# Gate and up projections of a feed-forward layer by seven products of half-block sums, tokens on partitions, with the hidden layer kept in DRAM

## The chip, the cores and the metric

The kernel runs on one core of a Trainium2 chip. A core has TensorE for matmuls (PE in the profile, with PEld for its weight loads), VectorE (DVE), ScalarE (ACT), GpSimd (POOL) and SyncE (SP), each with an instruction stream of its own; semaphores tie the streams together. SBUF is the on-chip memory of 128 partitions, PSUM holds matmul results in eight banks of 128 x 512 floats. The metric is device time in microseconds, taken as the median of several executions.

## What is computed

One layer of a decoder on 512 tokens of width 2048, all in float32: RMSNorm, an input projection, four token mixers side by side, an output projection added to the residual, then RMSNorm, a SwiGLU feed-forward of width 5632 and a last RMSNorm. The change lies in the feed-forward and in the last part of the output projection, which prepares its input.

```python
D_MODEL = 2048; SEQ = 512
D_FF = -(-8 * D_MODEL // (3 * 256)) * 256          # 5632
...
def rmsnorm(x, g):
    xf = x.astype(jnp.float32)
    y = xf * lax.rsqrt(jnp.mean(xf * xf, axis=-1, keepdims=True) + NORM_EPS)
    return (y * g.astype(jnp.float32)).astype(x.dtype)
...
        x = x + ycat.reshape(B, S, D_MIX) @ w_out[l]
        h = rmsnorm(x, norm_ffn_g[l])
        x = x + swiglu(h, w_gate[l], w_up[l], w_down[l])
    return rmsnorm(x, norm_final_g)
```

`swiglu(h, g, u, d)` is (silu(h @ g) * (h @ u)) @ d.

## The kernel before

A float32 product is made of three matmuls of a shorter format (F32R): each operand is cut into a high part (a copy on ScalarE that rounds) and a low part (a subtraction on VectorE), and high x high, high x low and low x high are summed in PSUM. Activations have features on partitions and the 512 tokens along the free axis; a tile of 128 x 512 floats comes from one pool of 79 slots (`t2`).

Weights come as one stream of 512 KB chunks in the order of use (`chunks`). `next_chunk` hands out the next one and, before that, issues the loads on SP's queue up to three chunks ahead (`issue_dma`) and the splits up to two ahead (`issue_split`: L122 on ScalarE, L123 on VectorE). A step of `gemm` takes a chunk of 512 input by 256 output features; for each of two blocks of 128 outputs and four slices of the input it gives three matmuls of 128x512, weights stationary and tokens moving (L162, L163, L164). A chunk is thus 24 matmuls. When a block's sum is complete, `on_block` drains it. `gemm_tok` (L180 to L182) is the same with tokens stationary and 512 weights moving. `run` drives these steps, and after each one it lets every generator in the list `side` advance by one step: that is how norms, attention and other side work get their place in the streams. Nothing is reordered later: each engine does what the code issues for it, in that order, with waits where tiles demand them.

The output projection runs in two parts, since the last mixer (attention of mixer A) is still at work: first branches 3, 1 and 2 (`gemm(3, rhs_y, add_x2)`), then branch 0 in eight pairs of blocks of one chunk each. There `split_x2` adds the product to the residual x2 on VectorE (L1030), makes the scaled high part `fh` on ScalarE (L1032), and, one block late, the low part `fl` on VectorE (L1041) and the square on ScalarE (L1047); `add_squares` (L1052) sums squares on VectorE. `ffn_norm` makes 1/rms of each token, spread over a tile R2.

The feed-forward takes the 44 hidden blocks of 128 in groups of eight (the last has four). For each block, `gemm(4, rhs_f, on_gu)` makes gate and up, 96 matmuls, and `on_gu` drains them: gate times R2 on VectorE (L1085), Silu on ScalarE (L1086), up times R2, their product, and the high and low part of it. After a group's blocks `gemm(n // 4, rhs_h, on_dn)` adds the group's share of down to x2, which stays in SBUF. The last group of down is mixed with the final norm, by halves of the tokens.

Of the kernel before, what the change touches and what calls it, by code (L numbers as in the profile page):

```python
# [39 lines left out]
def hybrid_kernel(ctx, tc, xT, wi, wt, wo, wgu, wdn, vec, rows, sgw, w2a2, g2, pbias, cmask, oneh, addc, out):  # L40
# [6 lines left out]
    p1 = ctx.enter_context(tc.tile_pool(name="p1", bufs=8))  # L47
# [7 lines left out]
    def th(name, shape=(128, 4, C)):  # L55
        return p1.tile(list(shape), F32, name=name, tag="sh", bufs=14)

    def t1(name, shape=(128, 8), dt=F32):
        return p1.tile(list(shape), dt, name=name, tag="s1")
# [20 lines left out]
    for g in range(8):  # L80
        chunks.append(wo[g, 0])
    ffg = []
# [5 lines left out]
    for b0, n in ffg:  # L88
        for b in range(b0, b0 + n):
            for kq in range(4):  # L90
                chunks.append(wgu[b, kq])
# [4 lines left out]
    st = dict(dma=0, split=0, use=0)  # L96
    PF, SP = 3, 2

    def issue_dma():
        i = st["dma"]  # L100
        if i >= len(chunks):
            return
# [4 lines left out]
    def issue_split():  # L107
        i = st["split"]
        if i >= len(chunks):
            return  # L110
# [29 lines left out]
    def next_chunk():  # L140
# [3 lines left out]
        while st["dma"] <= min(i + PF + ahead, len(chunks) - 1):  # L144
            issue_dma()
        while st["split"] <= min(i + SP - 1 + ahead, len(chunks) - 1):
# [22 lines left out]
    def gemm_tok(on_tok):  # L169
        """512 output features by all tokens, tokens on partitions; K = 2048."""  # L170
# [49 lines left out]
    class RowNorm:  # L220
        """1 / rms over features, for token columns of feature-major tiles."""
# [68 lines left out]
    def d_block(j, acc):  # L290
        """scale by 1/rms and shift by a token; block j of the RWKV input."""
# [29 lines left out]
    def rwkv_pre():  # L321
# [16 lines left out]
        # decay and in-context learning rate  # L338
# [132 lines left out]
    def turned(name, w):  # L471
        """the transpose of w for each of 8 heads."""
# [8 lines left out]
    def each_head(name, w, m):  # L481
        """w^T m for each of 8 heads (64 x 64 tiles)."""
# [72 lines left out]
    def rwkv_fin(c, gm, LT, dX):  # L555
        """(I - L)^-1 transposed, token-major B|K."""
# [48 lines left out]
    def rwkv_post(c, py3):  # L605
        """group norm per head, bonus, gate."""
# [181 lines left out]
    def attention(mix, br):  # L788
# [11 lines left out]
        class Head:  # L800
# [16 lines left out]
            def scores(self, i):  # L817
                """exp(scores - max) of the 128 queries of block i with their keys."""
# [19 lines left out]
            def turn(self, js):  # L838
                """the weights of key blocks js with keys on partitions."""
# [167 lines left out]
    x2 = []  # L1007
    for g in range(8):
        for b in range(2):
            x2.append(t2("x2"))  # L1010
            nc.scalar.dma_start(x2[-1], xT[:, 2 * g + b, :])
# [5 lines left out]
        def add_x2(b, acc, g=g):  # L1017
            dv.tensor_add(x2[2 * g + b], acc, x2[2 * g + b])
# [5 lines left out]
    fh, fl = [], []  # L1024
    norm2 = RowNorm()
    late = []
# [12 lines left out]
    def low_x2(j):  # L1039
        fl.append(t2("flo", dt=F32R))  # L1040
        dv.scalar_tensor_tensor(fl[j], x2[j], vcol(V_NFG + j), fh[j].bitcast(F32), op0=OP.mult, op1=OP.subtract)  # L1041

    sqs = []

    def square_x2(j):
        sqs.append(t2("sq"))
        ac.activation(sqs[-1], x2[j], AF.Square)  # L1047
# [5 lines left out]

    def ffn_norm():
        while len(sqs) > 1:
            for _ in range(2):
                add_squares()
            yield
# [3 lines left out]
        ac.activation(R2, norm2.spread(), AF.Copy)  # L1062

    for g in range(8):
        run(gemm(1, lambda c, k: (yh[0, k], yl[0, k]),
                 lambda b, acc, g=g: split_x2(g, b, acc)))
    for f in range(4):
        del yh[0, f], yl[0, f]
    R2 = R1

# [1 line left out]
    def rhs_f(c, k):  # L1072
        kt = 4 * c + k
        return fh[kt], fl[kt]

    first = True
    for gi, (b0, n) in enumerate(ffg):
        hh, hl = [], []
        for b in range(n):
            hold = {}  # L1080

            def on_gu(u, acc, b=b, hold=hold):
                if u == 0:
                    gs = hold["g"] = t2("gs")
                    dv.tensor_mul(gs, acc, R2)  # L1085
                    ac.activation(gs, gs, AF.Silu)  # L1086
                    return
                us = t2("us")
                dv.tensor_mul(us, acc, R2)
                dv.tensor_mul(us, us, hold["g"])  # L1090
# [156 lines left out]
```

## Time and profile before

| | us |
|---|---|
| median of 3 runs (2400.09 to 2404.08) | 2400.27 |
| span of the profiled execution | 2402.2 |
| input projection and mixers | 0 to 722.5 |
| output projection, branches 3, 1, 2 | 722.5 to 905.5 |
| output projection, branch 0 (eight pairs of blocks) | 905.5 to 949 |
| feed-forward | 949 to 2343 |
| last group of down and final norm | 2343 to 2402.2 |
| PE busy | 2382.8 (99%) |
| DVE busy | 1038.0 (43%) |
| ACT busy | 702.6 (29%) |

Busy is time with an instruction at work; matmuls overlap in the pipeline, so their distance from start to start is shorter than the length of one. The granted clock stands in the rows as a share of TensorE's full speed.

### The profile page before, as it was taken

Reading aid. Unit: us, or ns where it says so; the run is one execution under the profiler, and the core shown is the slowest. Engines: PE = TensorE matmul, PEld = TensorE weight load, DVE = VectorE, ACT = ScalarE, POOL = GpSimd, SP = SyncE. Lnnn points to the kernel's source line nnn. Section 1 sums busy time; section 2 is a strip of 40 time slices with the busy share of each in tenths; the row PEclk is TensorE's granted clock in tenths of the full one; section 3 lists DMA queues with packets and bytes.
Section 4 is the critical chain, followed back from the end, with each engine's and each line's share of the span. In section 5 each row is a group of like instructions: output and inputs, shape, how many; then the busy total and the mean of one; then the engine's idle time right before and its main releaser. Section 6 shows DMA issues by size and latency. Waiting matters only on the chain.

```text
span 2402.2 us, 28139 instructions
## 1 busy us (share of the span) xinstructions
PE 2382.8 (99%) x11760; PEld 1938.9 (81%) x11760; DVE 1038.0 (43%) x1564; ACT 702.6 (29%) x1016; POOL 2.3 (0%) x16
## 2 busy tenths in 40 slices
PE   8999999999999999999999999999999999999997
PEld 6788878777777778888888888888888888888887
DVE  6555445554445447333333333333333333333337
ACT  5522221225445445222122222222122212222223
POOL 0000000000000000000000000000000000000000
PEclk9999999989999999999999999999999999999999
DMA  5222313213223232233222222232223222322232
GB/s 182 87 89 79 101 56 89 68 53 97 75 75 122 89 105 97 95 98 97 97 97 97 97 97 97 97 98 99 98 93 103 98 97 89 105 97 97 90 120 89
DMA packets 83440, 228.38 MB, mean 95 GB/s; under 512 B 20400, under 2 KB 26032, under 8 KB 83312
## 3 DMA queue, kind: packets, MB, share of 16 engines
q1 hardware_dynamic: 77552, 216.30, 27.6%
q10 hardware_dynamic: 5760, 10.28, 1.4%
q8 instruction: 92, 1.51, 0.2%
q14 instruction: 36, 0.29, 0.0%
HBM read 221.53 MB, written 5.02 MB: 94 GB/s over the span
## 4 chain that ended last, share of the span: by engine, by line
PE 98%; DMA 1%; DVE 1%; ACT 0%; issue 0%; SPq 0%; DVEq 0%
PE acc L162 27%; PE acc L164 26%; PE acc L163 26%; PE acc L180 3%; PE acc L181 2%; PE acc L182 2%; PE po L895 1%; PE psc L830 1%; PE ppt L845 1%; DMA xraw<-in_xT_dram 1%; PE pg L520 1%; PE acc L1153 1%; PE psc L829 1%; PE acc L1154 1%; PE acc L1152 1%; PE py L682 1%
## 5 line engine op out<-in xcount | busy, mean ns | idle before, releaser
L123 DVE TENSOR_TENSOR wlo<-wraw,whi 128x1024 fp32r<-128x1024 f32 x383 | 469.0, 1225 | 784.6 <-ACT whi L122 784.3
L122 ACT ACTIVATE whi<-wraw 128x1024 fp32r<-128x1024 f32 x383 | 404.9, 1057 | 1040.2 <-PE acc L163 834.2
L162 PE MATMUL acc<-fhi,whi 128*128 128x512 f32 x1408 | 548.1, 389 | 0.0
L164 PE MATMUL acc<-fhi,wlo 128*128 128x512 f32 x1408 | 547.9, 389 | 0.0
L163 PE MATMUL acc<-flo,whi 128*128 128x512 f32 x1408 | 547.9, 389 | 0.0
L162 PEld LDWEIGHTS acc<-fhi,whi 128*128 128x128 f32 x1408 | 264.4, 188 | 54.8
L163 PEld LDWEIGHTS acc<-flo,whi 128*128 128x128 f32 x1408 | 264.4, 188 | 54.7
L164 PEld LDWEIGHTS acc<-fhi,wlo 128*128 128x128 f32 x1408 | 264.4, 188 | 54.7
L162 PE MATMUL acc<-hhi,whi 128*128 128x512 f32 x640 | 249.0, 389 | 0.0
L164 PE MATMUL acc<-hhi,wlo 128*128 128x512 f32 x640 | 249.0, 389 | 0.0
L163 PE MATMUL acc<-hlo,whi 128*128 128x512 f32 x640 | 249.0, 389 | 0.0
L162 PE MATMUL acc<-xhi,whi 128*128 128x512 f32 x512 | 211.9, 414 | 4.9 <-ACT whi L137 4.9
L163 PE MATMUL acc<-xlo,whi 128*128 128x512 f32 x512 | 202.8, 396 | 0.7 <-DVE xlo L253 0.7
L164 PE MATMUL acc<-xhi,wlo 128*128 128x512 f32 x512 | 202.8, 396 | 0.6 <-DVE wlo L123 0.6
L163 PEld LDWEIGHTS acc<-hlo,whi 128*128 128x128 f32 x640 | 120.2, 188 | 24.9
L164 PEld LDWEIGHTS acc<-hhi,wlo 128*128 128x128 f32 x640 | 120.2, 188 | 24.9
L162 PEld LDWEIGHTS acc<-hhi,whi 128*128 128x128 f32 x640 | 120.2, 188 | 24.9
L162 PEld LDWEIGHTS acc<-xhi,whi 128*128 128x128 f32 x512 | 97.8, 191 | 30.6 <-ACT whi L137 5.6
L164 PEld LDWEIGHTS acc<-xhi,wlo 128*128 128x128 f32 x512 | 97.8, 191 | 22.9 <-DVE wlo L123 1.8
L163 PEld LDWEIGHTS acc<-xlo,whi 128*128 128x128 f32 x512 | 98.1, 192 | 22.0 <-DVE xlo L253 2.0
L180 PE MATMUL acc<-whi,xhi 128*128 128x512 f32 x256 | 105.2, 411 | 0.0
L162 PE MATMUL acc<-yhi,whi 128*128 128x512 f32 x256 | 103.7, 405 | 0.0
(247 smaller groups left out, 2225.3 us busy)
## 6 DMA issues: line engine op xcount, KB each, us to landing
wraw<-in_wgu_dram SPq DMA_DIRECT2D x176, 512.0 KB, 3.4
wraw<-in_wdn_dram SPq DMA_DIRECT2D x88, 512.0 KB, 3.4
wraw<-in_wi_dram SPq DMA_DIRECT2D x63, 512.0 KB, 3.5
wraw<-in_wt_dram SPq DMA_DIRECT2D x32, 512.0 KB, 3.5
wraw<-in_wo_dram SPq DMA_DIRECT2D x32, 512.0 KB, 3.4
xraw<-in_xT_dram SPq DMA_DIRECT2D x16, 256.0 KB, 5.7
E<-tdram ACTq DMA_DIRECT2D x16, 256.0 KB, 3.6
x<-in_xT_dram ACTq DMA_DIRECT2D x16, 256.0 KB, 2.8
```

The lines of the kernel that those rows point to most:

```text
L122: ac.activation(hi, r, AF.Copy)
L123: dv.tensor_sub(lo, r, hi.bitcast(F32))
L162: pe.matmul(acc[b], wh, xh, start=(c == 0 and k == 0), stop=False)
L163: pe.matmul(acc[b], wh, xl, start=False, stop=False)
L164: pe.matmul(acc[b], wl, xh, start=False, stop=(c == nchunk - 1 and k == 3))
L180: pe.matmul(acc[i], th_, hi[:, k], start=(c == 0 and k == 0), stop=False)
L181: pe.matmul(acc[i], th_, lo[:, k], start=False, stop=False)
L182: pe.matmul(acc[i], tl, hi[:, k], start=False, stop=(c == 7 and k == 1))
L520: pe.matmul(p3[:, u, :], rw.BK[h // 2][q4][rr, ci].rearrange("p a t -> p (a t)"), rw.RA[h // 2][q4][rr, ci].rearrange("p a t -> p (a t)"), ...
L682: pe.matmul(py3[o, h // 2, :], rw.RA[h // 2][c // 4][o, c % 4, 0, :], St[o, h // 2, :], start=False, stop=True)
L829: pe.matmul(o, qs[:, cc], ks[:, 0:n], start=True, stop=False)
L830: pe.matmul(o, qs[self.rr, cc], kl[self.rr, 0:n], start=False, stop=True)
```

## The change

Gate and up are multiplied by Strassen's scheme with seven products of half-size blocks in place of eight. The tokens are cut into two halves of 256, the input features into two halves of eight tiles, and gate and up are the two column halves. Their sums are formed once for the tokens (`combine`, `late_sums`) and for each group of 512 hidden features for the weights (`w_sum`). A product has 256 tokens stationary (two 128-token tiles) and 512 weights moving, over eight tiles of input features: 48 matmuls (L1235 to L1237) in four steps of 12. Eleven groups by seven products by four steps are listed in `steps`; products P1, P6 and P7 go into one chain of PSUM sums. `w_ahead` issues loads, sums and splits of weights two to eight steps ahead. `got_product` drains each product's two token tiles into partial sums; behind P4 the gated second half of the tokens is ready, behind P2 the first half. It now has tokens on partitions, so `turn_h` transposes it on TensorE in two sets of four, copies each on ScalarE and stores it to DRAM (`hd`) from ScalarE's queue. Down then is a stage of its own, which loads h (`load_h`) and x2 (`load_x2`) back and splits h.

In the last part of the output projection, `make_x2` takes the place of `split_x2`: add, scaled copy, store of x2 to DRAM (`xd`) from ScalarE's queue, and a Square that overwrites the tile of x2. Pairs of blocks are now j and j + 8, for which the layout of the weights is changed.

```diff
@@ last part of the output projection
-    def split_x2(g, b, acc):
-        j = 2 * g + b
-        dv.tensor_add(x2[j], acc, x2[j])
-        fh.append(t2("fhi", dt=F32R))
-        ac.activation(fh[j], x2[j], AF.Copy, scale=vcol(V_NFG + j))
-        if j:
-            low_x2(j - 1)
-            square_x2(j - 1)
-        if j % 2:
-            add_squares()
...
+    def make_x2(j, acc):
+        dv.tensor_add(x2[j], acc, x2[j])
+        xg[j] = t2("xg")
+        ac.activation(xg[j], x2[j], AF.Copy, scale=vcol(V_NFG + j))
+        nc.scalar.dma_start(xd[j], x2[j])
+        sqs.append(x2.pop(j))
+        ac.activation(sqs[-1], sqs[-1], AF.Square)
+
+    def split2(hi, src, lo):
+
+        ac.activation(hi, src, AF.Copy)
+        dv.tensor_sub(lo, src, hi.bitcast(F32))
+
+    def combine(j):
+
+        a, b = xg[j], xg[j + 8]
+        s12, s34 = t2("s12"), t2("s34")
+        dv.tensor_add(s12[:, lo_t], a[:, hi_t], b[:, hi_t])
+        dv.tensor_sub(s12[:, hi_t], s12[:, lo_t], a[:, lo_t])
+        gp.tensor_sub(s34[:, lo_t], a[:, lo_t], a[:, hi_t])
+        gp.tensor_sub(s34[:, hi_t], b[:, lo_t], s12[:, hi_t])
+        a11 = t2("a11", dt=F32R)
+        split2(a11[:, lo_t], a[:, lo_t], a11[:, hi_t])
+        h12, l12 = t2("h12", dt=F32R), t2("l12", dt=F32R)
+        split2(h12, s12, l12)
...
+    def late_sums():
+        for _ in range(2):
+            yield
+        for j in range(8):
+            h34, l34 = t2("h34", dt=F32R), t2("l34", dt=F32R)
+            split2(h34, xg.pop(j), l34)
...
+    ORDER = ("P1", "P5", "P6", "P3", "P7", "P4", "P2")
...
+    steps = [(gi, p, jj) for gi in range(NGR) for p in ORDER for jj in range(4)]
...
+    def w_split(k):
+        gi, p, jj = steps[k]
+        hi = wp.tile([128, 2, 512], F32R, name="wh", tag="wraw", bufs=3)
+        lo = wp.tile([128, 2, 512], F32R, name="wl", tag="wsp", bufs=4)
...
+    def w_ahead(k):
+
+        w_dma(k + 4)
+        while sw["add"] < min(k + 4, len(steps)):
+            if sw["add"] >= sw["dma"]:
+                w_dma(sw["add"] + 1)
+            w_sum(sw["add"])
+            sw["add"] += 1
+            if sw["split"] < min(k + 3, sw["add"]):
+                w_split(sw["split"])
+                sw["split"] += 1
+        while sw["split"] < min(k + 3, len(steps)):
+            w_split(sw["split"])
+            sw["split"] += 1
+        w_dma(k + 8)
...
+    def turn_h(gi, th, h):
+
+        for b in range(2):
+            p = px("ph")
+            for fb in range(2):
+                for t in range(2):
+                    pe.transpose(p[:, fb * HT + t * 128:fb * HT + t * 128 + 128],
+                                 h[t][:, (2 * b + fb) * 128:(2 * b + fb + 1) * 128], ident)
+            o = t2("hT")
+            ac.activation(o, p, AF.Copy)
+            nc.scalar.dma_start(hd[4 * gi + 2 * b:4 * gi + 2 * b + 2, :, th * HT:(th + 1) * HT].rearrange("f p t -> p f t"),
+                                o.rearrange("p (f t) -> p f t", f=2))
+            yield
...
+        def gated(g, u, i):
+            ac.activation(g, g, AF.Silu, scale=norm2.r[:, i:i + 1])
+            dv.scalar_tensor_tensor(g, u, norm2.r[:, i:i + 1], g, op0=OP.mult, op1=OP.mult)
...
+        else:
+            c = part["c11", t]
+            dv.tensor_add(c, acc, c)
+            gated(c, part.pop(("c12", t)), t)
+            if t:
+                side.append(turn_h(gi, 0, [part.pop(("c11", 0)), part.pop(("c11", 1))]))
...
+                pe.matmul(acc[t], ah[:, tt], hi[:, u], start=first, stop=False, skip_group_check=more)
+                pe.matmul(acc[t], ah[:, tt], lo[:, u], start=False, stop=False, skip_group_check=more)
+                pe.matmul(acc[t], al[:, tt], hi[:, u], start=False, stop=(j == 7), skip_group_check=more)
+                if j == 7:
+                    got_product(gi, p, t, acc[t])
...
+        def on_last(b, acc, g=g):
+            make_x2(g + 8 * b, acc)
+            if b:
+                combine(g)
+            if g + b:
+                add_squares()
...
+    for k in range(len(steps)):
+        if k == len(steps) - 10:
+            side.append(load_h(*ffg[0]))
+        if k == len(steps) - 2:
+            st["end"] = len(chunks)
+            issue_dma()
+        run(strassen(k))
+    finish_all()
+    side.append(load_x2())
```

What stands in the streams, word for word, with the semaphores that an instruction waits for. TensorE before, where one block of gate and up ends and the next begins; `fhi` and `flo` are the tokens, `whi` and `wlo` the weights:

```order
L162 MATMUL acc_7841<-fhi,whi 128x512
L163 MATMUL acc_7841<-flo,whi 128x512
L164 MATMUL acc_7841<-fhi,wlo 128x512
L162 MATMUL acc_7960<-fhi,whi 128x512 [waits Activation_49]
L163 MATMUL acc_7960<-flo,whi 128x512
L164 MATMUL acc_7960<-fhi,wlo 128x512 [waits DVE_49]
```

TensorE now, where the first group's P2 ends and the second group's P1 begins; `c_7767` and `c_7772` are the two gated token tiles, `ph` the PSUM tile of the transposes, `cm` holds the identity:

```order
L1235 MATMUL prod<-wh,hb 128x512
L1236 MATMUL prod<-wl,hb 128x512
L1237 MATMUL prod<-wh,lb 128x512
L1177 MATMUL ph<-cm,c_7767 128x128 [waits DVE_49]
L1177 MATMUL ph<-cm,c_7772 128x128 [waits DVE_49]
L1177 MATMUL ph<-cm,c_7767 128x128
L1177 MATMUL ph<-cm,c_7772 128x128
L1235 MATMUL prod<-wh,a_7218 128x512 [waits Activation_49]
L1236 MATMUL prod<-wl,a_7218 128x512
L1237 MATMUL prod<-wh,a_7218 128x512
```

Between the last matmul of a product and the first of the next there are now four transposes that wait for VectorE; before, the next matmul waited for the split of its weights alone. VectorE before, at the same kind of place, with the drain of gate (`gs`) and up (`us`) between two weight splits:

```order
L123 TENSOR_TENSOR wlo<-wraw,whi 128x1024 [waits DMAHW5_49,PE_49,Activation_49]
L1085 TENSOR_TENSOR gs<-acc_7828,R_76 128x512 [waits PE_49]
L1089 TENSOR_TENSOR us<-acc_7841,R_76 128x512 [waits PE_49]
L1090 TENSOR_TENSOR us<-us,gs 128x512 [waits DVE_49,Activation_49]
L1094 TENSOR_TENSOR hlo<-us,hhi 128x512 [waits Activation_49]
L123 TENSOR_TENSOR wlo<-wraw,whi 128x1024 [waits DMAHW6_49,Activation_49]
```

VectorE now, behind the P4 of the first group (`c_8845` and `c_8851` are here the gate's two token tiles, `rn` the 1/rms of the tokens, `wl` low parts of weights):

```order
L1055 TENSOR_TENSOR wl<-wq,wh 128x512 [waits Activation_49] x4
L1206 TENSOR_TENSOR c_8845<-c_8845,prod 128x512 [waits PE_49]
L1193 SCALAR_TENSOR_TENSOR c_8845<-c_8576,rn,c_8845 128x512 [waits Activation_49]
L1206 TENSOR_TENSOR c_8851<-c_8851,prod 128x512 [waits PE_49]
L1193 SCALAR_TENSOR_TENSOR c_8851<-c_8583,rn,c_8851 128x512 [waits Activation_49]
L1055 TENSOR_TENSOR wl<-wq,wh 128x512 [waits DVE_49,Activation_49]
```

The subtraction of the second token tile stands behind the multiply of the first, which waits for ScalarE's Silu. ScalarE before, in the last part of the output projection, one pair of blocks between two weight splits:

```order
L122 ACTIVATE whi<-wraw 128x1024 [waits DMAHW4_49,PE_49,Activation_49]
L1032 ACTIVATE fhi<-x_6200,vc 128x512 [waits DVE_49]
L1047 ACTIVATE sq<-x_6023 128x512
L1032 ACTIVATE fhi<-x_6202,vc 128x512 [waits DVE_49]
L1047 ACTIVATE sq<-x_6200 128x512
L122 ACTIVATE whi<-wraw 128x1024 [waits DMAHW5_49,PE_49,Activation_49]
```

ScalarE now, one pair of blocks at the same place (`xd` is x2 in DRAM, `a` and `h` the high parts of token sums):

```order
L122 ACTIVATE whi<-wraw 128x1024 [waits DMAHW3_49,PE_49]
L1047 ACTIVATE xg<-x_6025,vc 128x512 [waits DVE_49]
L1048 DMA xd<-x_6025 128x512 [waits DMAHW1_49]
L1050 ACTIVATE x_6025<-x_6025 128x512 [waits DMAHW1_49,Activation_49]
L1047 ACTIVATE xg<-x_6027,vc 128x512 [waits DVE_49]
L1048 DMA xd<-x_6027 128x512
L1050 ACTIVATE x_6027<-x_6027 128x512 [waits DMAHW2_49,Activation_49]
L1054 ACTIVATE a_7275<-xg 128x256
L1054 ACTIVATE h_7278<-s_7269 128x512 [waits DVE_49]
L122 ACTIVATE whi<-wraw 128x1024 [waits DMAHW4_49,PE_49]
```

The Square (L1050) now waits for a semaphore of a DMA queue, behind the store of the same tile, and the next weight split stands behind both Squares.

## Rows read from the trace of the kernel before

**Rows 1.** The page's chain of work that ended last, shares of the span by line.

```profile
PE acc L162 27%; PE acc L164 26%; PE acc L163 26%; PE acc L180 3%; PE acc L181 2%; PE acc L182 2%; PE po L895 1%; PE psc L830 1%; PE ppt L845 1%; DMA xraw<-in_xT_dram 1%; PE pg L520 1%; PE acc L1153 1%; PE psc L829 1%; PE acc L1154 1%; PE acc L1152 1%; PE py L682 1%
```

**Rows 2.** Busy time by stage: stretch, length, engines (instructions), TensorE's clock, DMA share, GB/s.

```profile
905.50:949.00 43.50, 43.50 (x194) 36.03 (x193) 33.23 (x46) 25.73 (x38) 0.00 (x0) 1.00 0.30 97
949.00:2343.00 1394.00, 1394.00 (x6164) 1155.30 (x6163) 498.95 (x527) 326.95 (x354) 0.00 (x0) 1.00 0.30 98
```

**Rows 3.** TensorE's timeline: start, length, engine, line, operation, shape, count; two stretches.

```profile
1039.70 0.39 PE L162 MATMUL acc<-fhi,whi 128*128 128x512 f32 x1
...
1042.42 0.39 PE L162 MATMUL acc<-fhi,whi 128*128 128x512 f32 x1
...
715.06 0.39 PE L180 MATMUL acc<-whi,xhi 128*128 128x512 f32 x1
...
717.78 0.39 PE L180 MATMUL acc<-whi,xhi 128*128 128x512 f32 x1
```

**Rows 4.** TensorE's timeline around the eight transposes of attention at 753 us.

```profile
753.31 1.03 PE L845 MATMUL ppt<-cm,s 128*128 128x128 f32 x8
754.10 0.48 PE L162 MATMUL acc<-yhi,whi 128*128 128x512 f32 x1
754.41 0.40 PE L163 MATMUL acc<-ylo,whi 128*128 128x512 f32 x1
```

**Rows 5.** Groups by line and shape: count, busy us, mean ns, idle before, releaser.

```profile
L122 ACT ACTIVATE whi<-wraw 128x1024 fp32r<-128x1024 f32 x383 | 404.9, 1057 | 1040.2 <-PE acc L163 834.2 <-issue 131.2 <-PE acc L181 72.6
...
L1085 DVE TENSOR_TENSOR gs<-acc,R 128x512 f32<-128x512 f32 x44 | 30.4, 691 | 27.1 <-PE acc L164 27.1
...
L1047 ACT ACTIVATE sq<-x 128x512 f32<-128x512 f32 x16 | 9.8, 617 | 0.0
...
L786 ACT ACTIVATE avt<-acc,rn 128x512 f32<-128x512 f32 x8 | 5.5, 690 | 5.1 <-PE acc L182 5.1
```

**Rows 6.** Timeline of all engines where one block's gate is drained.

```profile
1054.44 0.39 PE L164 MATMUL acc<-fhi,wlo 128*128 128x512 f32 x1
...
1054.86 0.69 DVE L1085 TENSOR_TENSOR gs<-acc,R 128x512 f32<-128x512 f32 x1 [0.63 <-PE acc L164]
...
1055.59 0.63 ACT L1086 ACTIVATE gs<-gs 128x512 f32<-128x512 f32 x1 [2.61 <-DVE gs L1085]
```

**Rows 7.** VectorE's timeline in the last part of the output projection.

```profile
912.21 1.23 DVE L123 TENSOR_TENSOR wlo<-wraw,whi 128x1024 fp32r<-128x1024 f32 x1 [1.60 <-ACT whi L122]
913.36 0.68 DVE L1030 TENSOR_TENSOR x<-acc,x 128x512 f32<-128x512 f32 x1
913.96 0.74 DVE L1041 SCALAR_TENSOR_TENSOR flo<-x,vc,fhi 128x512 fp32r<-128x512 f32 x1
```

**Rows 8.** DMA issues: queue, operation, count, KB each, median us to landing.

```profile
x<-in_xT_dram ACTq DMA_DIRECT2D x16, 256.0 KB, 2.8
out_dram<-o SPq DMA_DIRECT2D x16, 256.0 KB, 2.3
```

**Rows 9.** TensorE's timeline around thin work, two stretches.

```profile
451.82 0.50 PE L162 MATMUL acc<-xhi,whi 128*128 128x512 f32 x1
...
511.50 0.33 PE L680 MATMUL py<-UV,gm 128*64 128x64 f32 x2
...
515.60 0.80 PE L180 MATMUL acc<-whi,xhi 128*128 128x512 f32 x1
...
519.10 0.39 PE L182 MATMUL acc<-whi,xlo 128*128 128x512 f32 x1
```

**Rows 10.** TensorE by stretch: length, busy (instructions), granted clock, DMA share, GB/s.

```profile
515.00:517.50 2.50, 2.50 (x11) 0.61 0.49 182
...
450.00:452.50 2.50, 2.50 (x19) 1.00 0.12 29
```

**Rows 11.** TensorE's timeline near the start, where a matmul waits for a weight split.

```profile
22.03 0.50 PE L164 MATMUL acc<-xhi,wlo 128*128 128x512 f32 x1 [0.21 <-DVE wlo L123]
22.37 0.40 PE L162 MATMUL acc<-xhi,whi 128*128 128x512 f32 x1
```

More of the change, by code (lines that the diff above doesn't have):

```diff
@@ L81, in hybrid_kernel @@
         chunks.append(wo[g, 0])
+    n_mix = len(chunks)
     ffg = []
@@ L88, in hybrid_kernel @@
     for b0, n in ffg:
-        for b in range(b0, b0 + n):
-            for kq in range(4):
-                chunks.append(wgu[b, kq])
         for dp in range(8):
@@ L95, in hybrid_kernel @@
     raws, parts = {}, {}
-    st = dict(dma=0, split=0, use=0)
+    st = dict(dma=0, split=0, use=0, end=n_mix)
     PF, SP = 3, 2
@@ L100, in issue_dma @@
         i = st["dma"]
-        if i >= len(chunks):
+        if i >= st["end"]:
             return
@@ L108, in issue_split @@
         i = st["split"]
-        if i >= len(chunks):
+        if i >= st["end"]:
             return
@@ L143, in next_chunk @@
         ahead = 2 if i + SP >= len(chunks) - 8 else 0
-        while st["dma"] <= min(i + PF + ahead, len(chunks) - 1):
+        while st["dma"] <= min(i + PF + ahead, st["end"] - 1):
             issue_dma()
-        while st["split"] <= min(i + SP - 1 + ahead, len(chunks) - 1):
+        while st["split"] <= min(i + SP - 1 + ahead, st["end"] - 1):
             issue_split()
@@ new lines, in hybrid_kernel, with w_dma, w_sum @@
+    RAWS = 12
+    def w_dma(limit):
+        while sw["dma"] < min(limit, len(steps)):
+            gi, p, jj = steps[sw["dma"]]
+            if p in FRESH:
+                if len(raw) + 2 > RAWS:
+                    return
+                kh, f = FRESH[p]
+                for j in (2 * jj, 2 * jj + 1):
+                    t = raw[kh, f, j] = t2("wq")
+                    nc.sync.dma_start(t, wgu[gi, kh, f, j])
+            sw["dma"] += 1
+    def w_sum(k):
+        gi, p, jj = steps[k]
+        js = (2 * jj, 2 * jj + 1)
+        if p == "P5":
+            T[jj] = fp.tile([128, 2, 512], F32, name="T")
+            for u, j in enumerate(js):
+                dv.tensor_sub(T[jj][:, u], raw.pop((0, 1, j)), raw.pop((0, 0, j)))
+            src[k] = T[jj]
+        elif p == "P6":
+            for u, j in enumerate(js):
+                dv.tensor_sub(T[jj][:, u], raw[1, 1, j], T[jj][:, u])
+            src[k] = T[jj]
+        elif p == "P4":
+            for u, j in enumerate(js):
+                dv.tensor_sub(T[jj][:, u], T[jj][:, u], raw[1, 0, j])
+            src[k] = T.pop(jj)
+        elif p == "P7":
+            for j in js:
+                dv.tensor_sub(raw[1, 1, j], raw[1, 1, j], raw.pop((0, 1, j)))
@@ new lines, in w_ahead @@
+    def w_ahead(k):
[12 more added lines that the diff above has]
+        w_dma(k + 8)
+    part = {}
@@ new lines, in hybrid_kernel, with strassen @@
+    bank = {}
+    def strassen(k):
+        gi, p, jj = steps[k]
+        w_ahead(k)
+        hi, lo = cut.pop(k)
+        chain = p in ("P1", "P6", "P7")
+        key = "U" if chain else p
+        if jj == 0 and p not in ("P6", "P7"):
+            bank[key] = [(px if p in ("P3", "P4") else pm)("prod") for _ in range(2)]
+        acc = bank[key]
+        for u in range(2):
+            j = 2 * jj + u
+            more = p in ("P6", "P7")
+            first = j == 0 and p not in ("P6", "P7")
+            ah, al = cmb[p, j]
+            for t in range(2):
+                tt = slice(t * 128, t * 128 + 128)
+                pe.matmul(acc[t], ah[:, tt], hi[:, u], start=first, stop=False, skip_group_check=more)
[3 more added lines that the diff above has]
+                    got_product(gi, p, t, acc[t])
+            if gi == NGR - 1:
+                del cmb[p, j]
+            del ah, al
+            yield
+        if jj == 3 and p not in ("P1", "P6"):
+            del bank[key]
```

151 lines of the change are left out of this document (98 added, 53 removed).

## The prediction

> **What bounds the kernel now.** I read the chain of work that ended last first: by line, 86% of it is TensorE's six matmul lines in the two helpers [rows 1]. The busy time by stage then says where: from 905.5 to 2343 us, the output projection's last part and the whole feed-forward, TensorE's column equals the length of the stretch, while VectorE is busy 33.2 of 43.5 us in the first and 499 of 1394 us in the second [rows 2]. So a matmul that goes is worth its spacing, and work for VectorE or ScalarE costs nothing until TensorE has to wait for it. The spacing is in the timeline: twelve 128x512 matmuls in 2.72 us, 0.2267 us each, with weights stationary, and the same with tokens stationary and weights moving [rows 3]. The 0.39 us in a row is one matmul's length in the pipeline, not its price.
>
> **Removed.** Gate and up had 44 blocks x 4 chunks x 24 = 4224 matmuls; now 11 groups x 7 products x 48 = 3696. 528 x 0.2267 = **119.7 us** less. Down keeps its matmuls.
>
> **Added on TensorE: transposes.** Per group two pairs of four for each half of the tokens: 176 of 128x128, in 44 sets of four. Eight such stood 0.79 us in the stream, and the matmul behind took 0.31 instead of 0.23 [rows 4]: 4 x 0.10 + 0.08 = 0.48 us a set, **+21 us** (18 to 23).
>
> **Added wait 1: the transposes wait for the gate.** In the new order the four transposes stand directly behind the last matmul of the fourth and of the second product, 22 times, and the next product's matmuls stand behind them. VectorE's order there is subtract, multiply, subtract, multiply, with a Silu on ScalarE ahead of each multiply, so the second token half starts only after the first half's multiply. Counting from the start of the first half's last matmul: it ends at 0.39, and VectorE follows 0.03 later (matmul 1054.44, VectorE 1054.86), ScalarE 0.04 after VectorE's end [rows 6]. Subtract out of PSUM 0.69, Silu with a column as scale 0.70 (the scaled drain on ScalarE took 0.69) [rows 5], multiply 0.74 [rows 7]: first multiply done at 0.42 + 0.69 + 0.04 + 0.70 + 0.04 + 0.74 = 2.63. Then the same again without the matmul, 0.69 + 0.04 + 0.70 + 0.04 + 0.74 = 2.21, with VectorE's next start some 0.06 early: 4.8. TensorE would have gone on at 0.91; less the one transpose that runs meanwhile, 3.86 us of standstill. 22 x 3.86 = **+85 us** (75 to 92: with the hops gone, or with one split of 0.6 us in the queue ahead). Behind the waiting transposes the whole of TensorE's queue stands; on VectorE, sums and splits of coming steps stand behind the multiply, but they are three steps (8 us) ahead.
>
> **Added wait 2: x2 is written out and overwritten in place.** In the last part of the output projection each block now gives ScalarE a scaled copy, a DMA of x2 to DRAM, and a Square that overwrites x2. The Square waits for that DMA, and everything ScalarE has behind it too, the split of the next weight chunk among it. VectorE's running sum of squares waits for the Square, the next block's add stands behind that sum. No row of before shows ScalarE waiting for its own store; a 256 KB store landed in 2.3 us at the end of the kernel, a 256 KB load on ScalarE's queue in 2.8 [rows 8]; I take the store. The issue itself is counted as part of the landing. One pair of blocks, from the start of one chunk's low split to the next: low split 1.15 to the next start [rows 7], add 0.69, scaled copy to Square 2.35, Square 0.62, sum of squares 0.60, add 0.69, copy to Square 2.35, Square 0.55, two splits 0.35 and 0.55 (half a tile and a whole one, estimated from the Square's 0.62), chunk split 1.05 and five hops of 0.04: 11.1 us against 24 x 0.2267 = 5.44 of matmuls (durations [rows 5, 6, 7]). Measured from the first pair's last matmul, the low split of the third chunk starts at 5.8; five more pairs 55.3; then 1.15, 10.2 for the seventh pair (no chunk split behind it) and 10.9 for the eighth up to the first gate weights' low split: 83.4 us where before 38.1 passed. **+45 us** (53 with 2.8 us landings; 18 if the landing were hidden, since 16 x 1.7 us of it go).
>
> **Small items, +8 us** (3 to 18). Group 0 also splits the late token sums on VectorE, 16 x 0.6 us beside steps that already hold up to 2.4 of 2.72 us: some 3 us. At the start of down the transposed h, its store and the first chunk's split stand in a row on ScalarE: 0.6 + 0.6 + 1.05, then 1.23 for the low part [rows 5, 7]: 3.6 us. The rest is a table load and the split of the first h. Gate and up now load 40 tiles a group in place of 32, and h and x2 go out and in; 0.30 of the DMA engines' time was used [rows 2], and all loads are issued two steps or more ahead, so I cost this at nothing. VectorE's splits and sums are 61 us per group at back-to-back starts (0.60 and 1.15 us [rows 7]) against 76 us of matmuls: hidden.
>
> **The clock.** After 4.1 us of thin 64-column work from 511.50, matmuls came 0.43 us apart, eight from 515.60 to 519.10 [rows 9], and the granted clock of that window was 0.61, mostly the lower level of 1.2 GHz; the same work up to 451.82 left it at 1.00, 2.4 GHz [rows 9, 10]. Eight matmuls at 0.43 lose 1.7 us. The 22 standstills, 4.3 us with their transposes, lie just there: 0 to 37 us. I take a third, **+13 us**.
>
> **Sum:** -119.7 + 21 + 85 + 45 + 8 + 13 = +52 on the profiled execution's 2402.2 us. That one is 1.9 above the median of the three runs (2400.27), so on the median: **2453 us**.
>
> **Rivals.**
> *R1, every pause lowers the clock.* The full 37 in place of 13: 2477. For it: 515.60. Against it: 451.82 [rows 9, 10]. The Trainium skill ("TensorE: Matmul & The Clock Gate", HAM oscillation) tells of a kernel whose matmul groups each wait and each then start at the lower clock; by that every one of the 22 would lose, and the two rows agree with it only half.
> *R2, the store is no wait.* If the Square need not wait for the landing, or it lands at once, 45 becomes 18: 2426.
> *R3, faster: the matmuls behind the waiting transposes go on.* They need other banks and operands that are ready. Then the 85 and the clock's 13 go: 2355. It decides where a standstill falls under (119.7 - 21 - 45 - 8) / 22 = 2.1 us. Against it: at 22.03 a matmul waited for a low split, and the next one, which needed only the high part, came after it [rows 11]. The Trainium skill (the same page, Step-by-step) has only weight loads pulled forward and matmuls in program order; the row agrees.
> *R4, VectorE becomes the bound in gate and up.* If its starts are as far apart as its durations (0.69), the eight steps around the fifth product hold 8 x 4 x 0.69 + 4 x 0.69 = 24.8 us against 21.8 of matmuls: 11 x 3 = 33 more, 2487. Against it: back-to-back starts of 0.60 [rows 7].
> That the change doesn't do what it says is excluded: the order holds 3696 matmuls of the new form.
>
> **How the numbers follow.** Forecast 0.53 (its bounds: 2430 to 2475), R1 0.17, R2 0.14, R4 0.10, R3 0.06. Leaving out R3 and the far ends, 2420 to 2495 holds about 8 in 10. A measurement of this kernel tells 0.2% (4.8 us) from no change. Faster: R3, 0.06. Within 0.2% needs standstills of about 2 us: 0.03. Slower 0.91.
>
> **What would show it.** The profile of after should show: matmuls of the new form 0.227 us apart inside a product; TensorE idle 22 times for some 2 and then 2 us at the transposes, released by VectorE's multiply; ScalarE's Square waiting about 1.7 us on a DMA 16 times and pairs of blocks 11 us apart; VectorE below 85% busy in gate and up. Transposes that wait under 2 us, or pairs 5.5 us apart, would make the forecast wrong.

## The result, and the profile after

The changed kernel takes 2483.69 us (median of four runs, 2476.71 to 2485.02), the one before 2400.18: a ratio of 1.0343, interval 1.0325 to 1.0361. It is 83.5 us slower; 2453 was forecast, with a range of 2420 to 2495.

The profiled execution has a span of 2482.9 us against 2402.2, so 80.7 more. The busy time by stage says where. Columns as in [rows 2]; the stretches are the last part of the output projection up to the first product, the products, and the change to down.

```profile
905.50:997.20 91.70, 54.03 (x183) 39.27 (x181) 41.18 (x68) 34.42 (x56) 11.69 (x16) 0.79 0.33 103
997.20:1977.70 980.50, 906.09 (x3872) 738.84 (x3872) 712.51 (x1014) 456.70 (x681) 0.00 (x0) 0.96 0.41 129
1977.70:1985.40 7.70, 1.48 (x9) 0.89 (x8) 2.32 (x4) 3.71 (x6) 0.00 (x0) 0.82 0.45 144
```

The first line answers to the first of [rows 2]: there TensorE's column filled the stretch, here 37.7 of 91.7 us are empty. TensorE's timeline has the first matmul of branch 0 and the first one of the feed-forward, before and then after:

```profile
903.62 0.39 PE L162 MATMUL acc<-yhi,whi 128*128 128x512 f32 x1
...
947.14 0.39 PE L162 MATMUL acc<-fhi,whi 128*128 128x512 f32 x1
```

```profile
902.91 0.39 PE L162 MATMUL acc<-yhi,whi 128*128 128x512 f32 x1
...
997.17 0.79 PE L1235 MATMUL prod<-wh,a 128*128 128x512 f32 x1 [14.59 <-ACT wh L1054]
```

The first feed-forward matmul starts at 997.17 where it started at 947.14 before: **+50.0 us**. The stage itself takes 94.26 us in place of 43.52, 50.7 more; the stages ahead of it, which the change leaves alone, end 0.7 us sooner here. Their end moves by up to 9 us between the profiled executions of this document (894.4 to 903.6), so below the length of a stage is given beside its start. In the second line 3696 product matmuls would take 3696 x 0.2267 = 837.9 us; it holds 980.5. Against the 4224 x 0.2267 = 957.6 us of gate and up before, that is **+22.9**. The third line has no counterpart before: **+7.7**. Down takes 484.0 us from its first matmul to its last, as it did before, so the loads of h and x2 back from DRAM cost nothing. 50.0 + 22.9 + 7.7 = 80.6.

The list of waits (engine, line, released by: us in all, times, longest) names the two that were forecast:

```profile
PE ph L1177 <- DVE c L1193: 77.2, 44, 2.8
...
ACT x L1050 <- DMA xd<-x: 31.8, 16, 4.1
```

One standstill, at the end of the first group's P4, in the timeline of TensorE, VectorE and ScalarE (start, length, engine, line, operation, idle time before and its releaser):

```profile
1068.04 0.69 DVE L1206 TENSOR_TENSOR c<-c,prod 128x512 f32<-128x512 f32 x1
1068.29 0.39 PE L1237 MATMUL prod<-wh,lb 128*128 128x512 f32 x1
1068.76 0.72 ACT L1192 ACTIVATE c<-c,rn 128x512 f32<-128x512 f32 x1 [0.31 <-DVE c L1206]
1069.52 0.75 DVE L1193 SCALAR_TENSOR_TENSOR c<-c,rn,c 128x512 f32<-128x512 f32 x1 [0.79 <-ACT c L1192]
1070.19 0.68 DVE L1206 TENSOR_TENSOR c<-c,prod 128x512 f32<-128x512 f32 x1
1070.32 0.33 PE L1177 MATMUL ph<-cm,c 128*128 128x128 f32 x1 [1.64 <-DVE c L1193]
1070.90 0.72 ACT L1192 ACTIVATE c<-c,rn 128x512 f32<-128x512 f32 x1 [1.42 <-DVE c L1206]
1071.66 0.75 DVE L1193 SCALAR_TENSOR_TENSOR c<-c,rn,c 128x512 f32<-128x512 f32 x1 [0.79 <-ACT c L1192]
1072.46 0.90 PE L1177 MATMUL ph<-cm,c 128*128 128x128 f32 x3 [1.81 <-DVE c L1193]
1073.02 0.78 PE L1235 MATMUL prod<-wh,hb 128*128 128x512 f32 x1
1073.59 0.63 PE L1236 MATMUL prod<-wl,hb 128*128 128x512 f32 x1
```

VectorE's second subtraction at 1070.19 has had its product since 1068.68, and stands behind the first multiply. There are two waits for VectorE, 1.64 and 1.81 us, with one transpose between them. From the last product matmul's turn (1068.29 + 0.23) to the next product at 1073.02 there are 4.50 us; 21 such gaps sum to 93.9, 4.47 each. The matmuls behind it stand 0.57 and then 0.43 us apart. TensorE's granted clock in that stretch and in the next five microseconds (length, busy, clock, DMA share, GB/s):

```profile
1073.00:1078.00 5.00, 5.00 (x16) 0.50 0.38 113
1078.00:1083.00 5.00, 5.00 (x24) 1.00 0.64 206
```

So after each standstill TensorE works for a while at the lower level, 1.2 GHz. Over all products 146 starts come more than 0.07 us late, 31 us together. Not all of that is the standstills' doing: in e2 below, which has none of the 21, 58 starts and 8 us remain.

In the last part of the output projection the Square waits for the store of x2. ScalarE's timeline, one pair of blocks (ACTq is the issue of the DMA):

```profile
916.36 0.72 ACT L1047 ACTIVATE xg<-x,vc 128x512 f32<-128x512 f32 x1 [2.15 <-DVE x L1045]
916.36 0.33 ACTq L1048 DMA_DIRECT2D xd<-x  x1
920.46 0.63 ACT L1050 ACTIVATE x<-x 128x512 f32<-128x512 f32 x1 [3.38 <-DMA xd<-x]
922.45 0.72 ACT L1047 ACTIVATE xg<-x,vc 128x512 f32<-128x512 f32 x1 [1.36 <-DVE x L1045]
922.46 0.33 ACTq L1048 DMA_DIRECT2D xd<-x  x1
924.54 0.63 ACT L1050 ACTIVATE x<-x 128x512 f32<-128x512 f32 x1 [1.37 <-DMA xd<-x]
```

The chain of work in this stretch (905 to 1000 us), by line, puts 44.7% on these stores:

```profile
by line: DMA xd<-x 44.7%; issue 14.4%; DVE x L1040 10.5%; DVE x L1045 10.3%; ACT x L1050 7.8%; ACT h L1054 4.5%; ACT a L1054 3.0%; DVE l L1055 1.1%; PE prod L1236 0.8%; DVE wl L1055 0.7%; PE acc L164 0.5%; PE prod L1237 0.4%; PE prod L1235 
```

Chunk splits on ScalarE are first 12.7 to 13.0 us apart (913.17, 925.91, 938.95, 951.66), then 10.7 to 10.8 (962.40, 973.18).

### The profile page after: what moved, and what is told of

It is laid out like the page before. It is cut to its first block, busy times and chain, and to the rows that moved or that the text cites. A ratio compares the mean times of both kernels' runs of the same rounds, so it can differ in the third digit from the quotient of the medians.

```text
span 2482.9 us, 29487 instructions
## 1 busy us (share of the span) xinstructions
PE 2345.5 (94%) x11404; PEld 1889.9 (76%) x11404; DVE 1439.3 (58%) x2278; ACT 949.8 (38%) x1487; POOL 14.0 (1%) x32
## 4 chain that ended last, share of the span: by engine, by line
PE 90%; DVE 4%; ACT 2%; DMA 2%; issue 1%; SPq 0%; ACTq 0%; DVEq 0%
PE acc L162 13%; PE acc L164 12%; PE acc L163 12%; PE prod L1236 11%; PE prod L1235 11%; PE prod L1237 11%; PE acc L180 3%; PE acc L181 2%; PE acc L182 2%; DMA xd<-x 2%; DVE c L1193 1%; ACT c L1192 1%; PE ph L1177 1%; PE po L895 1%; PE psc L830 1%
## 5 line engine op out<-in xcount | busy, mean ns | idle before, releaser
L123 DVE TENSOR_TENSOR wlo<-wraw,whi 128x1024 fp32r<-128x1024 f32 x207 | 253.1, 1223 | 304.6 <-ACT whi L122 304.3
L122 ACT ACTIVATE whi<-wraw 128x1024 fp32r<-128x1024 f32 x207 | 218.7, 1057 | 547.1 <-PE acc L163 434.3
L1055 DVE TENSOR_TENSOR wl<-wq,wh 128x512 fp32r<-128x512 f32 x352 | 227.2, 687 | 175.3 <-ACT wh L1054 175.2
L1054 ACT ACTIVATE wh<-wq 128x512 fp32r<-128x512 f32 x352 | 202.8, 624 | 228.5 <-PE prod L1237 165.0
L1235 PE MATMUL prod<-wh,h 128*128 128x512 f32 x704 | 273.9, 389 | 0.0
L1236 PE MATMUL prod<-wl,h 128*128 128x512 f32 x704 | 273.9, 389 | 0.0
L1237 PE MATMUL prod<-wh,l 128*128 128x512 f32 x704 | 273.9, 389 | 0.0
L1055 DVE TENSOR_TENSOR wl<-T,wh 128x1024 fp32r<-128x1024 f32 x132 | 161.4, 1223 | 49.9 <-ACT wh L1054 49.9
L1235 PEld LDWEIGHTS prod<-wh,h 128*128 128x128 f32 x704 | 132.1, 188 | 27.6
L1237 PEld LDWEIGHTS prod<-wh,l 128*128 128x128 f32 x704 | 132.1, 188 | 27.3
L1235 PE MATMUL prod<-wh,hb 128*128 128x512 f32 x352 | 145.6, 414 | 0.0
L1236 PE MATMUL prod<-wl,hb 128*128 128x512 f32 x352 | 142.9, 406 | 0.0
L1237 PE MATMUL prod<-wh,lb 128*128 128x512 f32 x352 | 142.7, 405 | 0.0
```

The source lines that it names most:

```text
L122: ac.activation(hi, r, AF.Copy)
L123: dv.tensor_sub(lo, r, hi.bitcast(F32))
L1054: ac.activation(hi, src, AF.Copy)
L1055: dv.tensor_sub(lo, src, hi.bitcast(F32))
L1235: pe.matmul(acc[t], ah[:, tt], hi[:, u], start=first, stop=False, skip_group_check=more)
L1236: pe.matmul(acc[t], ah[:, tt], lo[:, u], start=False, stop=False, skip_group_check=more)
```

## The experiments

Each is the changed kernel with the edit shown; times are medians, ratios against the kernel before in the same series. Differences from the changed kernel's median go across series, in which the kernel before took 2396.2 to 2400.2 us; lengths of stages come from the profiled executions.

### e1: the Square writes a tile of its own

```diff
-        sqs.append(x2.pop(j))
-        ac.activation(sqs[-1], sqs[-1], AF.Square)
+        sqs.append(t2("sq"))
+        ac.activation(sqs[-1], x2.pop(j), AF.Square)
```

> The Square of x2 writes a tile of its own, so it need not wait for the store of x2. Theory (the store's landing sets the pace of the last part of the output projection): its 16 waits, 31.8 us in the changed kernel, go; pairs of blocks fall from 10.8 to 12.7 us to about 7.7; of the 50.0 us by which the first product starts late, 27 to 32 go: 2452 to 2457. Rival A (the order alone sets the pace: scaled copies, sums and splits of a pair stand in front of the next chunk's split, and the wait lies beside them): under 8 us, 2476 or more. Rival B (the slot of x2 comes free later, and the next writer of it waits for the store in place of the Square): under 8 us too, with waits of VectorE or ScalarE on the store at another line.

Measured: 2451.42 us (2448.17 to 2455.92), ratio 1.0217 (1.0190 to 1.0243): 32 us less than the changed kernel. The first product starts at 967.84 in place of 997.17, and the stage takes 66.25 us in place of 94.26, 28.0 less. Pairs of blocks are 8.2 us apart. ScalarE's timeline shows the Square right behind the scaled copy:

```profile
921.73 0.72 ACT L1047 ACTIVATE xg<-x,vc 128x512 f32<-128x512 f32 x1 [2.26 <-DVE x L1045]
921.73 0.33 ACTq L1048 DMA_DIRECT2D xd<-x  x1
922.36 0.62 ACT L1050 ACTIVATE sq<-x 128x512 f32<-128x512 f32 x1
```

What remains against the kernel before, 66.25 - 43.52 = 22.7 us, is the order of the work of a pair; the forecast's second rival had put that at 18. Both rivals of this run are refuted by the 28.0.

### e2: the transposes 24 matmuls later

```diff
     def turn_h(gi, th, h):
-
+        for _ in range(4):
+            yield
         for b in range(2):
```

> The transposes of h stand 24 matmuls (5.4 us) later, inside the next product. Theory (22 standstills, each 3.9 us of waiting and 1.3 us of matmuls at the lower clock behind it): 22 x 3.9 = 86 and some 31 go, 2365 to 2372. Rival A (the matmuls 0.43 us apart behind a standstill have another cause than the pause, such as the transposes themselves): the 31 stay, 2398. Rival B (VectorE is the bound of gate and up once TensorE no longer waits): about 33 us come back as waits of the products for the splits of weights, 2398 to 2405, and then TensorE is seen idle in front of product matmuls, released by VectorE's or ScalarE's split.

Measured: 2364.69 us (2362.94 to 2366.71), ratio 0.9860 (0.9838 to 0.9881): 119 us less than the changed kernel, and 1.4% faster than the kernel before. The products take 864 us in place of 980.5, 116 less; the wait that is left is the last group's, which has no product behind it:

```profile
PE ph L1178 <- DVE c L1194: 3.5, 2, 1.8
```

The busy time from 997 to 1859 us rules rival B out, that VectorE bounds the products: TensorE's column is full, VectorE's is at 705 of 862.

```profile
997.00:1859.00 862.00, 861.96 (x3869) 713.33 (x3870) 704.88 (x1010) 448.43 (x678) 0.00 (x0) 1.00 0.47 146
```

### e3: both edits

> Both edits together: the Square into a tile of its own, the transposes 24 matmuls later. Theory (the two costs lie in different stages and add up): 2484 less 29 less 115, 2340, which is 60 us under the kernel before. Rival (VectorE the bound in gate and up): 2370 to 2375.

Measured: 2336.23 us (2331.61 to 2340.84), ratio 0.9741 (0.9713 to 0.9769). The two costs add up: 2483.69 - 32.3 - 119.0 = 2332.

### e4: the standstill filled with matmuls

```diff
+    fill = []
...
+        fill.append(h12)
...
     def turn_h(gi, th, h):
+        pd = px("pd")
+        for _ in range(16):
+            pe.matmul(pd, fill[0][:, 0:128], fill[0], start=True, stop=True)
         for b in range(2):
```

> Each standstill is filled with 16 matmuls of 128x512 whose result nobody reads, ahead of the transposes; the wait stays as long as it is, and TensorE works through most of it. Theory (the matmuls 0.43 us apart behind a standstill are the lower clock that follows a pause): the 146 slow spacings in gate and up, 31 us, and some 5 us of slow transposes go, 2446 to 2455. Rival A (they have another cause): 2484. Rival B (the fill delays the transposes beyond the wait, since a fill of 3.6 us and the rest of the wait do not overlap fully): 2484 or more with the slow spacings gone.

Measured: 2447.13 us (2445.67 to 2450.87), ratio 1.0206 (1.0183 to 1.0228): 37 us less, though nothing was made shorter. The products take 947.8 us in place of 980.5, 33 less; in the profiled executions another 6.5 us come from the stages ahead, which the edit leaves alone. Late starts fall from 146 (31.4 us) to 61 (8.9 us); the other 10 us are transposes, which in the changed kernel run at the lower clock too. TensorE's timeline has the fill where the wait was, and the matmuls behind the transposes are at full pace; the granted clock of the stretch is 1.00:

```profile
1078.63 3.79 PE L1176 MATMUL pd<-h 128*128 128x512 f32 x16
1082.26 0.87 PE L1181 MATMUL ph<-cm,c 128*128 128x128 f32 x4
1082.88 0.48 PE L1239 MATMUL prod<-wh,a 128*128 128x512 f32 x1
```

```profile
1078.70:1086.70 8.00, 7.95 (x40) 1.00 0.22 71
```

That the slow matmuls come from the pause, and not from the transposes, is shown by this run: the transposes are there, the pause is not.

### e7: the drains in another row

```diff
-        def gated(g, u, i):
-            ac.activation(g, g, AF.Silu, scale=norm2.r[:, i:i + 1])
-            dv.scalar_tensor_tensor(g, u, norm2.r[:, i:i + 1], g, op0=OP.mult, op1=OP.mult)
+        def gated2(a, b, i0):
+            for t in range(2):
+                g = part[a, t]
+                ac.activation(g, g, AF.Silu, scale=norm2.r[:, i0 + t:i0 + t + 1])
+            for t in range(2):
+                g = part[a, t]
+                dv.scalar_tensor_tensor(g, part.pop((b, t)), norm2.r[:, i0 + t:i0 + t + 1], g, op0=OP.mult, op1=OP.mult)
...
             dv.tensor_sub(c, c, acc)
-            gated(c, part.pop(("c22", t)), 2 + t)
             if t:
+                gated2("c21", "c22", 2)
```

The subtraction stays ahead of `if t`, so both are done before either multiply; the first half of the tokens is treated alike.

> The changed kernel with the drains behind the fourth and second product in the row subtract, subtract, multiply, multiply in place of subtract, multiply, subtract, multiply; transposes where they are. Theory (each standstill is the chain on VectorE and ScalarE, worked out instruction by instruction): the second multiply ends 1.5 us earlier, standstills fall from 4.45 to about 2.95 us, 22 x 1.5 = 33 less, 2451; the matmuls at the lower clock behind each stay as many (another 0 to 25 less if the shorter pause spares them). Rival (the standstill hangs on the transposes' own start or on ScalarE's queue, not on the row of VectorE): within 8 us of 2484.

Measured: 2427.48 us (2423.70 to 2428.07), ratio 1.0114 (1.0099 to 1.0130): 56 us less. The gaps fell from 4.47 to 2.79 us, 1.7 each, and the second wait is short. TensorE's timeline, the two waits of one standstill:

```profile
1063.82 0.33 PE L1177 MATMUL ph<-cm,c 128*128 128x128 f32 x1 [1.64 <-DVE c L1197]
1064.50 0.57 PE L1177 MATMUL ph<-cm,c 128*128 128x128 f32 x3 [0.35 <-DVE c L1197]
```

So the row of VectorE does set the length, as worked out. Of 21 gaps (20 of 2.79 us, the last 4.08), 14 were followed by matmuls at full pace (two late starts, 0.2 us), 7, the last among them, by six or seven at the lower level (1.4 us); in the changed kernel, where the gaps are 4.2 to 5.7 us, all 21 were followed by six or more. The gaps give back 34 us (93.9 to 59.9) and the late starts 16 (31.4 to 15.5); the products with the change to down are 54.7 us shorter. In the profiled executions another 6.7 us come from the stages ahead, which the edit leaves alone.

### e5 and e6: work on x2 one chunk later, and a smooth change to down

e5 is e3 with the scaled copies, stores, Squares and sums of a pair issued one chunk later by a generator (`post`), and the first gate weights split earlier. e6 also splits down's first chunk ahead of the last product and leaves the last transposes to down's steps.

```diff
+    def post(g):
+        yield
+        for j in (g, g + 8):
+            make_x2(j)
+        yield
+        combine(g)
+        add_squares()
+        add_squares()
+        yield
...
         def on_last(b, acc, g=g):
-            make_x2(g + 8 * b, acc)
+            j = g + 8 * b
+            dv.tensor_add(x2[j], acc, x2[j])
             if b:
-                combine(g)
-            if g + b:
-                add_squares()
+                side.append(post(g))
...
+        if k == len(steps) - 1:
+            issue_split()
         run(strassen(k))
-    finish_all()
     side.append(load_x2())
```

> e3 with the work on x2 (scaled copy, store, Square, token sums, sum of squares) issued one chunk later, behind the split of the chunk after next, and the first gate weights split before the last pair is done. In e3 pairs of blocks are 8.24 us apart, with VectorE in the row add, wait for the copy, sums, wait for the split, sum of squares, wait for the Square. Theory (that row, not the amount of work, sets 8.24; the work of a pair is 4.5 us on ScalarE and 5.2 us on VectorE): pairs return to 5.44 to 5.7 us, the first product starts near 950 instead of 960.8, 2322 to 2327. Rival (VectorE's amount of work is the limit already, above all with GpSimd beside it on the same port of memory): pairs stay over 7 us, 2334 or more.

> e5 with a smooth change to down: its first chunk is split before the last product's matmuls end, and the last transposes are left to the steps of down instead of being finished first. In e3 7.9 us pass from the last product matmul to the first of down, in which 3.5 us are waits for the gate and 2.8 us for the split. Theory: 6 to 7.5 us less than e5. Rival (the load of h or x2 back from DRAM is what down waits for): under 2 us less, with waits on a DMA at the start of down.

Measured: e5 2323.80 us (2321.17 to 2329.33), ratio 0.9689 (0.9672 to 0.9706); e6 2314.64 us (2311.38 to 2316.46), ratio 0.9646 (0.9632 to 0.9660). In e5 the first product starts at 941.7, 19 us sooner than in e3 and after a stage of 47.2 us in place of 66.2, more than expected, but pairs are 6.48 us apart, not 5.44 to 5.7: here the rival holds in part. VectorE is now busy for 18.7 of the 20 us from 915, and its low split takes 1.77 us in place of 1.21 in the four pairs where GpSimd's subtraction had started before it. The two engines' timelines in e5:

```profile
921.34 1.11 POOL L1072 TENSOR_TENSOR s<-xg 128x256 f32<-128x256 f32 x1 [1.37 <-ACT xg L1056]
...
921.76 1.76 DVE L123 TENSOR_TENSOR wlo<-wraw,whi 128x1024 fp32r<-128x1024 f32 x1
```

Of the 19 us part is given back: the second norm's matmuls now stand in TensorE's stream before the sum of squares is done, a new wait of 8.6 us. In e6 the change to down takes 0.23 us, one matmul's spacing, 8.1 less than in e5.

### e8, e9, e10: what is left

e8 is e6 with eight transposes in a row; e9 is e8 with the norm's matmuls eight half-steps later; e10 is e9 with GpSimd's subtractions moved into the first products.

```diff
@@ e8
+        ph = [px("ph") for _ in range(2)]
         for b in range(2):
-            p = px("ph")
+            p = ph[b]
...
+        for b in range(2):
+            p = ph[b]
             o = t2("hT")
@@ e9
+        for _ in range(8):
+            yield
         norm2.add(sqs.pop(0))
@@ e10
-        gp.tensor_sub(s34[:, lo_t], a[:, lo_t], a[:, hi_t])
-        gp.tensor_sub(s34[:, hi_t], b[:, lo_t], s12[:, hi_t])
...
-            split2(h34, xg.pop(j), l34)
...
+            gp.tensor_sub(s34[:, lo_t], a[:, lo_t], a[:, hi_t])
+            gp.tensor_sub(s34[:, hi_t], b[:, lo_t], s12[:, hi_t])
+            yield
+            split2(h34, s34, l34)
```

> e6 with the eight transposes of a half in one row instead of two rows of four. Theory (a set costs 4 x 0.10 us and some 0.1 us for the change back to wide matmuls, and a tenth of a microsecond more per slow matmul behind it): 22 changes fewer, 2 to 6 us less than e6. Rival (eight transposes in a row are thin work long enough to lower the clock each time): 10 or more us above e6, with matmuls 0.43 us apart behind each set.

> e8 with the matmuls of the second norm issued eight half-steps later, behind 48 more product matmuls. In e8 they stand in TensorE's stream where the sum of squares is not yet done, and the stream waits 8.5 us there. Theory: these 8.5 us and some 2 us at the lower clock behind them go, 2300 to 2304, which is near 2400 - 120 + 24 for the transposes. Rival (the wait hides another one: the splits of the first products are late as well): 2306 or more, with TensorE waiting for a split of weights near 955 us.

> e9 with GpSimd's two subtractions per pair moved out of the last part of the output projection, to where their results are first split, inside the first products. In e5 and e9 VectorE's low split of a weight chunk took 1.77 us where GpSimd worked at the same time, and 1.21 us in e3 where it did not. Theory (the two engines slow one another down when they work at once, and VectorE's full 6.48 us per pair hold the pairs apart): the low split returns to 1.2 us, pairs to 5.6 to 5.9 us, the first product starts 3 to 5 us earlier, 2306 to 2309. Rival A (the 1.77 us have another cause, such as ScalarE's Square beside it): split and pairs stay, 2311. Rival B (the slow-down moves along to the first products, whose splits are already late): pairs shorten and the wait for splits there grows by as much, 2311.

Measured: e8 2311.84 us (2309.84 to 2315.64), ratio 0.9640 (0.9623 to 0.9656); e9 2311.33 (2306.39 to 2313.24), 0.9631 (0.9618 to 0.9644); e10 2313.39 (2310.21 to 2316.86), 0.9648 (0.9634 to 0.9662). The three cannot be told apart from one another or from e6. e8's rival, eight transposes that lower the clock, is refuted: the products take 869.9 us in place of 871.9 in e6. The theories of e9 and e10 failed, their rivals held. In e9 the norm's 8.5 us went and 3.5 us of waits for weight splits came, which the norm's wait had hidden; of the expected 8 to 12 us half a microsecond is seen in the medians and 4.5 in the profiled spans. In e10 the low split is back at 1.22 us and pairs at 5.84, and the stage is 2.5 us shorter than in e9, but the slowing moved along with GpSimd's work: waits for splits in the first products grew to 7.3 us. TensorE's waits, e9 and then e10:

```profile
PE prod L1251 <- DVE wl L1064: 3.5, 5, 1.8
```

```profile
PE prod L1254 <- DVE wl L1064: 7.3, 7, 2.4
```

e8 is the plainest of these three, 87 us under the kernel before in its series; e2 and e3, with far smaller edits, are faster than both kernels too. With only the transposes added, the forecast's own terms give 2400 - 120 + 21 = 2301.

## Why the prediction was right, and where its sizes were off

**Removed, 119.7.** Right. In e2 the products' spacing is 0.2267 us but for 58 late starts (8 us), the transposes and the first steps; 528 matmuls less are worth what the spacing says.

**Transposes, 21.** Right: in e2 and e3 a set of four costs 0.36 us up to the next matmul, and the start behind the set is 0.09 late: 44 x 0.45 = 20. In e8 eight in a row stood 0.79 us, as in [rows 4].

**Wait 1, the gate: 85.** Right, step by step. From the first half's last matmul (1067.61) to the end of the second multiply (1071.66 + 0.75) are 4.80 us, where 4.8 were worked out. 3.86 + 0.48 = 4.34 us were forecast from the last product matmul to the next product, 4.47 measured. Of the 0.13 more and of what the transposes took, some is the clock: with full-pace transposes, in e4, the same stretch is 4.26. e7 changed the row of VectorE and the length followed.

**Wait 2, the store: 45.** Right in kind, 6 low (50.7 for the stage, and 50.9 to 51.1 in e2, e4 and e7, which leave it alone). The pairs without a weight load beside the store took 10.7 to 10.8 us where 11.1 were worked out; three took 12.7 to 13.0, since the landing was 4 us there and not the 2.3 of [rows 8]. The load of a weight chunk is issued 0.6 us ahead of the first store of those pairs. Busy time with the first and the second store of one pair, the DMA share being the second column from the right:

```profile
916.40:920.40 4.00, 4.00 (x19) 3.30 (x18) 0.00 (x0) 0.68 (x1) 0.74 (x1) 1.00 0.69 197
922.50:924.50 2.00, 0.00 (x0) 0.00 (x0) 0.85 (x2) 0.67 (x1) 0.27 (x1) 0.98 0.35 131
```

Twice the DMA share, twice the landing. That the load is the cause was not tried on its own. The second rival, a store that is no wait, is refuted by the trace and by e1, and its price for the rest, 18, came out at 22.7.

**The clock, 13.** This is the step that was mis-sized: it measured 33. A third of 37 us was taken, because [rows 10] had one thin stretch that lowered the clock and one that did not. All the long standstills lowered it, and e4, which fills them, gives back 33 us in the products. R1 was the case that held, at 2477: the measured 2483.69 lies above the forecast's own bounds, 2430 to 2475, and in the wider range because that made room for R1. The weighing took thin matmul work as the pattern for a standstill. In a standstill TensorE does less, 1.04 us busy of the 4.50 from 1068.50; that this is why every one lost was not tried on its own. The Trainium skill ("TensorE: Matmul & The Clock Gate", HAM oscillation) describes groups of matmuls that each wait and each start at the lower clock, and by that every one of the 22 loses; the granted clock of 0.50 behind 1073 agrees with it, and e7's gaps of 2.79 us, of which 14 of 20 lost next to nothing, show that the length of the pause matters.

**Small items, 8.** The late token sums cost nothing that can be seen (in e2 the products hold no wait for them). The change to down took 7.7 us, with the last standstill in it, about as forecast for both.

**The sum.** Forecast +52, measured +80.7: 20 from the clock, 6 from the landings, the rest spread over the standstills. R3, matmuls going on past the waiting transposes, did not happen: none of the 44 waits was passed by a matmul. R4, VectorE as the bound, had put 2487, nearest of all to the measured time, and is refuted by e2: the right number can stand behind the wrong cause.

## What to carry to other kernels

An instruction that needs another engine's last result belongs some steps behind the work that makes it: here four empty steps of a generator, 5.4 us of other matmuls in between, were worth 119 us, as much as the 528 matmuls that the seven products save. A standstill of TensorE costs its length and, where it is long (here all of 4.1 us and more, 6 of 20 of 2.8 us), the slower matmuls behind it; work that overwrites a tile in place waits for whoever still reads it, here a store to DRAM (31.8 us in 16 waits). Cost the waits a change creates as carefully as the work it removes.

## What the runs showed of the hardware that was not expected

GpSimd and VectorE slow one another down when they work at once, and in e5 the order of their starts says which one. Six low splits of VectorE (128x1024) overlap a subtraction of GpSimd's (128x256, 0.73 us in the changed kernel). In four GpSimd had started first, and VectorE's took 1.77 us in place of 1.21; in two VectorE had started first, kept its 1.21 to 1.22 us, and GpSimd's took 1.16 and 1.51. One of these two:

```profile
909.12 1.21 DVE L123 TENSOR_TENSOR wlo<-wraw,whi 128x1024 fp32r<-128x1024 f32 x1
...
909.42 1.51 POOL L1072 TENSOR_TENSOR s<-xg 128x256 f32<-128x256 f32 x1 [1.37 <-ACT xg L1056]
```

e9 has the same six. In e10 one subtraction of GpSimd's stretched to 8.69 us while VectorE worked without a gap; lengths in GpSimd's rows are rough. GpSimd's line in e10, and VectorE's low split there, now alone:

```profile
962.11 8.69 POOL L1089 TENSOR_TENSOR s<-xg 128x256 f32<-128x256 f32 x1 [5.23 <-issue]
```

```profile
920.28 1.22 DVE L123 TENSOR_TENSOR wlo<-wraw,whi 128x1024 fp32r<-128x1024 f32 x1
```

The Trainium skill ("SBUF — State Buffer", SBUF: two separate sides) says that the two share a pair of ports as an exclusive lock, which the instruction that starts first holds for its whole length. The six cases of e5 agree with it; no run was made to separate it from another kind of sharing.

In the changed kernel ten of the 16 stores of x2, 256 KB each from ScalarE's queue, landed in 2.0 us, and the four with a load issued just ahead of them in 4.0 to 4.7 us.
